# A float32 encoder trunk: the weight tiles' splits are issued with two tiles in hand instead of one

## The chip, the cores and the metric

The kernel runs on one core of one Trainium2 chip. The metric is the device time of one execution in microseconds (us); where several executions were timed, their median is given. The core's engines are TensorE (PE in the profile, with its weight loads as PEld), VectorE (DVE), ScalarE (ACT), GpSimd (POOL) and SyncE (SP), which issues the transfers here.

## The reference

Two layers of a hybrid encoder run over 272 positions (256 tokens and 16 learned meta tokens) of width 2048, in float32. In each layer one projection `h @ w_in` gives queries, keys, values and gates for two groups of heads. Four heads do gated linear attention in both directions, with a decay that depends on the data. Sixteen heads do neighbourhood attention over a grid 64 wide, with the meta tokens as further keys. Both outputs go through `w_out`, a residual and a layer norm; then a squared-ReLU MLP of width 8192, a residual and a second layer norm follow:

```python
mix = jnp.einsum('blm,md->bld', jnp.concatenate([y_gla, y_na], axis=-1), w_out)
h = _layer_norm(DEEPNORM_ALPHA * h + mix, ln1_w, ln1_b)
ff = jnp.einsum('blf,fd->bld', jnp.square(jax.nn.relu(jnp.einsum('bld,df->blf', h, w_ff1))), w_ff2)
return _layer_norm(DEEPNORM_ALPHA * h + ff, ln2_w, ln2_b)
```

The meta tokens are dropped from the output. All weights together are read once from HBM, some 400 MB.

## The kernel before

The activations stand transposed in SBUF, features on the partitions and positions along the free dimension. Every large product is done in three matmuls of a rounded float32 type (fp32r): a weight tile w is split into a high part `wh` and the rest `wl`, the activations likewise into `xh` and `xl`, and wh·xh, wh·xl and wl·xh are added in PSUM.

**The weight stream.** `order` (L120) yields the 512 KB weight tiles (128 x 1024) in the order of their use, 768 in all. `made` (L137) brings in one: SP issues its transfer into `raw` (L146), ACT casts it to `wh` (L147), DVE subtracts to get `wl` (L148). `raw`, `wh` and `wl` each rotate over three buffers (the pool `wst`). So the `wh` and `wl` of a tile cannot be written before PE has done with the tile three earlier, and a tile's transfer not before the splits of the tile three earlier are done. `weights` (L131) is called each time a new tile is needed. It first fills the queue `ready` up to a count by calling `made`, then hands out the oldest. The very first tile comes in four parts and the second in two (`first` in L122).

**The two loops of matmuls.** `by_m` (L190) works on one block of 128 output features at a time, eight blocks of the contraction to a weight tile; the three matmuls are in `three` (L151; L160 to L162, or L156 and L157 where 256 positions allow xh and xl to go side by side in one matmul of 512 columns). `by_k` (L173) keeps four blocks of outputs in PSUM and goes along the contraction two blocks at a time, 24 matmuls to a weight tile (L186). It serves where activations come in one after another: at the start of the program (`load_x`, L291, loads and splits two blocks of x ahead of each tile), at the output projection, and after a layer norm (`normed`, L872, which calls `renew`, L877, to split the normalized blocks).

**Work in the background.** Attention, gates and layer norms are generators in two queues, `bg` and `fg`. `pump` (L104) moves them on by some steps after each weight tile. A step's instructions are traced inside `issue_after(self.wl)` (L98): what a step puts on DVE is kept behind the DVE instruction that made the latest `wl`. The linear attention of a head (`gla_head`, L437) goes through nine levels. For most of them POOL forms differences (L463), ACT exponentials (L468), DVE a product (L469), and PE small matmuls (L498, L493); copies under a mask (L515) gather the results. The gates' reciprocals (L423) and products (L426) run beside them on DVE.

**The order on the engines.** The program is written through a framework whose scheduler orders each engine's instructions by a model of its own. Engines run their lists in that order. On SP the order is that of the transfers' issue.

## Time and profile before

| | |
|---|---|
| median of 3 runs | 2422.17 us (2421.37 to 2422.31) |
| the profiled execution | 2421.64 us |
| its span, first to last instruction | 2419.7 us |
| granted TensorE clock | 0.999 |
| PE, PEld busy | 99%, 94% of the span |
| DVE, ACT, POOL busy | 65%, 49%, 12% |
| HBM traffic | 412.34 MB read, 171 GB/s over the span |

The span is the profiled execution's time without some 2 us around it. A busy share is the time in which at least one instruction of the engine ran. Rows of a timeline give the start and the duration in us, the engine and line, the operation, the tiles written and read, and in brackets the idle time before it and who ended it. Rows of the waits name who waited for whom, the sum in us, the number of waits and the longest.

### The profile page before, as it was taken

Reading aid. Unit: us, or ns where it says so; the run is one execution under the profiler, and the core shown is the slowest. Engines: PE = TensorE matmul, PEld = TensorE weight load, DVE = VectorE, ACT = ScalarE, POOL = GpSimd, SP = SyncE. Lnnn points to the kernel's source line nnn. Section 1 sums busy time; section 2 is a strip of 40 time slices with the busy share of each in tenths; the row PEclk is TensorE's granted clock in tenths of the full one; section 3 lists DMA queues with packets and bytes.
Section 4 is the critical chain, followed back from the end, with each engine's and each line's share of the span. In section 5 each row is a group of like instructions: output and inputs, shape, how many; then the busy total and the mean of one; then the engine's idle time right before and its main releaser. Section 6 shows DMA issues by size and latency. Waiting matters only on the chain.

```text
span 2419.7 us, 43687 instructions
## 1 busy us (share of the span) xinstructions
PE 2399.3 (99%) x17582; PEld 2265.2 (94%) x17582; DVE 1570.8 (65%) x2475; ACT 1191.4 (49%) x1980; POOL 287.2 (12%) x448
## 2 busy tenths in 40 slices
PE   9999999999999999999999999999999999999998
PEld 9999999999999999999999889998988888888887
DVE  6678777775544455546577787778866555666655
ACT  6555555564433344444456555555644333444444
POOL 1165320010000000000020444300200000000000
PEclk9999999999999999999999999999999999999999
DMA  7534444555555555555555444456556556555554
GB/s 240 166 132 152 141 139 157 173 176 176 175 177 175 176 175 175 175 174 174 175 169 185 140 154 158 137 156 199 183 185 190 186 189 188 186 189 186 187 188 139
DMA packets 118362, 417.28 MB, mean 172 GB/s; under 512 B 13388, under 2 KB 16460, under 8 KB 118160
## 3 DMA queue, kind: packets, MB, share of 16 engines
q1 hardware_dynamic: 118160, 414.49, 53.9%
q8 instruction: 138, 2.26, 0.4%
q14 instruction: 64, 0.52, 0.1%
HBM read 412.34 MB, written 2.10 MB: 171 GB/s over the span
## 4 chain that ended last, share of the span: by engine, by line
PE 94%; DVE 3%; ACT 1%; POOL 1%; issue 1%; DMA 0%; ACTq 0%; SPq 0%; POOLq 0%; DVEq 0%
PE mm L156 22%; PE mm L160 17%; PE mm L162 17%; PE mm L161 17%; PE mm L157 11%; PE mm L186 6%; POOL lev L463 1%; DVE wl L148 1%; PE bg L498 1%; PE bg L651 1%; PE bg L600 0%; PE bg L541 0%; PE bg L324 0%; PE bg L542 0%; DVE acc L870 0%
## 5 line engine op out<-in xcount | busy, mean ns | idle before, releaser
L148 DVE TENSOR_TENSOR wl<-raw,wh 128x1024 fp32r<-128x1024 f32 (+1 forms) x772 | 947.0, 1227 | 655.4 <-ACT wh L147 645.8
L147 ACT CAST wh<-raw 128x1024 fp32r<-128x1024 f32 (+1 forms) x772 | 805.2, 1044 | 949.8 <-PE mm L161 401.6
L160 PE MATMUL mm<-x,wh 128*128 128x272 f32 (+2 forms) x2176 | 632.3, 291 | 0.0
L162 PE MATMUL mm<-x,wl 128*128 128x272 f32 (+2 forms) x2176 | 628.0, 289 | 0.0
L161 PE MATMUL mm<-x,wh 128*128 128x272 f32 (+2 forms) x2176 | 627.7, 288 | 0.0
L160 PEld LDWEIGHTS mm<-x,wh 128*128 128x128 f32 x2176 | 412.7, 190 | 3.2 <-issue 0.4
L162 PEld LDWEIGHTS mm<-x,wl 128*128 128x128 f32 x2176 | 410.1, 188 | 0.3
L156 PE MATMUL mm<-x,wh 128*128 128x512 f32 x1152 | 409.6, 397 | 0.0
L161 PEld LDWEIGHTS mm<-x,wh 128*128 128x128 f32 x2176 | 409.4, 188 | 0.0
L157 PE MATMUL mm<-x,wl 128*128 128x256 f32 x1152 | 324.6, 282 | 0.4 <-DVE wl L148 0.4
L156 PEld LDWEIGHTS mm<-x,wh 128*128 128x128 f32 x1152 | 217.5, 189 | 50.8 <-issue 0.4
L156 PE MATMUL mm<-y,wh 128*128 128x512 f32 x688 | 242.1, 393 | 0.0
L157 PEld LDWEIGHTS mm<-x,wl 128*128 128x128 f32 x1152 | 217.4, 189 | 1.3 <-DVE wl L148 1.1
L162 PE MATMUL mm<-y,wl 128*128 128x272 f32 (+1 forms) x720 | 207.6, 288 | 0.0
L160 PE MATMUL mm<-y,wh 128*128 128x272 f32 (+1 forms) x720 | 207.5, 288 | 0.0
L161 PE MATMUL mm<-y,wh 128*128 128x272 f32 (+1 forms) x720 | 207.2, 288 | 0.0
L157 PE MATMUL mm<-y,wl 128*128 128x256 f32 x688 | 193.0, 281 | 0.5 <-DVE wl L148 0.5
L463 POOL TENSOR_TENSOR lev<-be 128x128 f32<-128x128 f32 (+1 forms) x256 | 162.3, 665 | 109.4 <-PE bg L498 32.1
L156 PE MATMUL mm<-u,wh 128*128 128x512 f32 x496 | 174.9, 393 | 0.0
L156 PEld LDWEIGHTS mm<-y,wh 128*128 128x128 f32 x688 | 128.8, 187 | 29.5
L162 PE MATMUL mm<-u,wl 128*128 128x272 f32 (+1 forms) x528 | 152.2, 288 | 0.0
L160 PE MATMUL mm<-u,wh 128*128 128x272 f32 (+1 forms) x528 | 152.2, 288 | 0.0
(266 smaller groups left out, 3305.5 us busy)
## 6 DMA issues: line engine op xcount, KB each, us to landing
raw<-in_wff SPq DMA_DIRECT2D x512, 512.0 KB, 3.5
raw<-in_win SPq DMA_DIRECT2D x190, 512.0 KB, 3.6
raw<-in_wout SPq DMA_DIRECT2D x64, 512.0 KB, 3.6
nb<-in_nab SPq DMA_DIRECT2D x16, 352.0 KB, 3.9
out<-acc SPq DMA_DIRECT2D x8, 256.0 KB, 2.6
xraw<-in_xT SPq DMA_DIRECT2D x7, 272.0 KB, 5.1
wraw<-in_wup SPq DMA_DIRECT2D x2, 392.0 KB
raw<-in_win SPq DMA_DIRECT2D x4, 128.0 KB, 3.0
```

What stands on the lines that cost most here:

```text
L147: nc.scalar.copy(wh[:, c], raw[:, c])
L148: self.wl = nc.vector.tensor_tensor(wl[:, c], raw[:, c], wh[:, c].bitcast(F32), ALU.subtract).ins
L156: mm(ps, lhsT=wh[:, c:c + P], rhs=x.both[:, :, :T], start=first, stop=False)
L157: mm(ps[:, T:], lhsT=wl[:, c:c + P], rhs=xh[:, :T], start=False, stop=last)
L160: mm(o, lhsT=wh[:, c:c + P], rhs=xh[:, :n], start=first, stop=False)
L161: mm(o, lhsT=wh[:, c:c + P], rhs=xl[:, :n], start=False, stop=False)
L162: mm(o, lhsT=wl[:, c:c + P], rhs=xh[:, :n], start=False, stop=last)
L186: self.nc.tensor.matmul(ps[m][:, :n], lhsT=parts[p][0][:, c:c + P], rhs=acts[j][parts[p][1]][:, :n], start=j + p == 0, stop=j == nk - 1 an ...
L463: tt = lambda o, x, y: nc.gpsimd.tensor_tensor(o, x, y, ALU.subtract)
L498: nc.tensor.matmul(ps[b * 64:b * 64 + 64, s * 64:s * 64 + 64], lhsT=k[:, c:c + 64], rhs=q[:, r:r + 64], start=True, stop=True)
L651: nc.tensor.matmul(r[hs], lhsT=(v2 if rest else v1)[:, t, hs], rhs=p2[:, t, :] if rest else p1[:, 2 * t + hh, :], start=rest, stop=not rest)
```

## The change

`weights` fills `ready` up to three tiles instead of two before it hands out the oldest. So when tile i is handed out, tile i+2 has had its transfer, its cast and its subtraction issued, where before it was tile i+1. Buffers and everything else are as they were.

```diff
     def weights(self):

-        while len(self.ready) < 2:
+        while len(self.ready) < 3:
             self.ready.append(self.made(*next(self.stream, (None, 0))))
         return self.ready.popleft()
```

In the order in which the two programs are built, no instruction is added and none is gone. At the start, SP issues the third weight tile ahead of the second pair of x blocks; before, it came behind it. On DVE, 148 of the 772 subtractions L148 have another place, 143 of them an earlier one, and what they overtake is work of the background. On PE, some 15 of the 72 groups of level matmuls (L498, L493) stand up to 28 matmuls later.

## The prediction

> **What bounds the kernel now.** I read the page first, for the engine that is never free and for the costs of the lines that the change moves.

> ```profile
> span 2419.7 us, 43687 instructions
> PE 2399.3 (99%) x17582; PEld 2265.2 (94%) x17582; DVE 1570.8 (65%) x2475; ACT 1191.4 (49%) x1980; POOL 287.2 (12%) x448
> L148 DVE TENSOR_TENSOR wl<-raw,wh 128x1024 fp32r<-128x1024 f32 (+1 forms) x772 | 947.0, 1227 | 655.4 <-ACT wh L147 645.8
> L147 ACT CAST wh<-raw 128x1024 fp32r<-128x1024 f32 (+1 forms) x772 | 805.2, 1044 | 949.8 <-PE mm L161 401.6
> ```

> PE is busy for all but 2419.7 - 2399.3 = 20.4 us. One tile's split costs ACT 1.04 us and DVE 1.23 us. So I asked next what PE waits for: the waits of PE, all rows, and one of its weight loads.

> ```profile
> PE mm L186 <- ACT wh L147: 4.8, 1, 4.8
> PE bg L498 <- DVE lev L469: 1.6, 2, 1.3
> PE bg L541 <- ACT Am L529: 1.3, 1, 1.3
> PE mm L186 <- DVE wl L148: 1.0, 1, 1.0
> PE mm L157 <- DVE wl L148: 0.9, 2, 0.5
> PE bg L636 <- DVE nv L628: 0.6, 2, 0.3
> PE bg L651 <- DVE p L641: 0.6, 1, 0.6
> PE bg L498 <- ACT lev L468: 0.5, 1, 0.5
> PE bg L523 <- DVE lev L482: 0.4, 1, 0.4
> PE bg L636 <- DVE ns L587: 0.4, 2, 0.2
> PE bg L493 <- DVE lev L469: 0.2, 1, 0.2
> PEld mm L157 <- DVE wl L148: 2.1, 3, 1.0
> ```

> The first row is the start of the program. The others sum to 7.5 us, and only 1.0 + 0.9 of it is a wait for a split. That is the size of the question: the whole prize is a few us in 2420. Last, the windows of the two MLP stretches, and who holds the splits up:

> ```profile
> 480.00:1235.00 755.00, 755.00 (x6004) 754.79 (x6003) 412.72 (x528) 329.83 (x459) 12.63 (x8) 1.00 0.55 175
> 1690.00:2404.00 714.00, 714.00 (x4268) 633.42 (x4267) 436.08 (x592) 321.65 (x432) 13.12 (x8) 1.00 0.58 184
> ACT wh L147 <- PE mm L161: 401.6, 231, 2.6
> ACT wh L147 <- PE mm L156: 243.7, 148, 2.8
> DVE wl L148 <- ACT wh L147: 645.8, 527, 3.8
> ```

> In 755 + 714 = 1469 us PE has no idle time at all (columns: length, then busy PE, PEld, DVE, ACT, POOL). And ACT's cast there waits for PE: it stands ready before PE has left the buffer, which is the tile three back. With three buffers the split already starts at the earliest moment that exists. Issuing it earlier changes nothing in these stretches; it can only act where DVE or ACT have other work in front of the split.

> **The change part by part.** No instruction is added; places change. There are four terms.

> *1. The start: +1.3 us.* SP now issues the third weight tile ahead of the second pair of x blocks. Timelines of SP and ACT before, and PE by windows (length, busy, count):

> ```profile
> 4.51 0.43 SPq L295 DMA_DIRECT2D xraw<-in_xT  x1
> 4.99 0.43 SPq L146 DMA_DIRECT2D raw<-in_win  x1
> 9.80 0.74 ACT L209 CAST x<-xraw 128x272 fp32r<-128x272 f32 x2 [0.88 <-DMA xraw<-in_xT]
> 11.10 1.05 ACT L147 CAST wh<-raw 128x1024 fp32r<-128x1024 f32 x1 [0.56 <-DMA raw<-in_win]
> 4.77:10.20 5.43, 5.42 (x24) 1.00 0.93 289
> 10.20:31.50 21.30, 21.30 (x170) 1.00 0.89 305
> ```

> The 24 matmuls of the first tile end at 10.2. The second tile's need the pair of blocks whose transfer ended ACT's wait at 9.80 and whose first cast is done at half of 0.74 us later, 10.2: just in time, with no slack. The weight tile behind it in the queue landed at 11.10. With the two swapped, the same bytes stand ahead of the pair, so I let it land when the tile did: PE's second tile starts 11.10 - 9.80 = 1.3 us later. No one makes that up, for PE then runs without a gap, at 21.30/170 = 125 ns a matmul. Bounds: 0, if the two transfers share the queue so that the pair lands as before; 2.4, if ACT's cast of that weight tile (1.05), which now stands ahead of the pair's casts, comes fully in the way as well (1.3 + 1.05). I take 1.3, the distance of the two landings. [...]

> *2. Splits that PE waits for in the attention and layer norm of the second layer: -1.5 us.* These two rows of PE's timeline are the row "0.9, 2" above:

> ```profile
> 1425.57 0.39 PE L157 MATMUL mm<-x,wl 128*128 128x256 f32 x1 [0.36 <-DVE wl L148]
> ...
> 1629.57 0.38 PE L157 MATMUL mm<-y,wl 128*128 128x256 f32 x1 [0.55 <-DVE wl L148]
> ```

> In the changed order these two subtractions stand 2.6 and 3.6 us of DVE's work earlier, which is more than the wait. So they go. They cost at least the idle time, 0.9, and at most the weight loads' wait, 2.1; I take the middle.

> *3. From the first layer to the second: 0.* Here DVE is saturated, and order alone cannot make time:

> ```profile
> 1261.52 1.21 DVE L148 TENSOR_TENSOR wl<-raw,wh 128x1024 fp32r<-128x1024 f32 x1
> ...
> 1265.63 0.99 DVE L210 TENSOR_TENSOR x<-acc,x 128x272 fp32r<-128x272 f32 x2
> 1268.64 0.78 DVE L210 TENSOR_TENSOR x<-acc,x 128x272 fp32r<-128x272 f32 x2
> 1269.35 1.43 DVE L148 TENSOR_TENSOR wl<-raw,wh 128x1024 fp32r<-128x1024 f32 x1
> ```

> PE's wait of 1.0 is for the last of these. In the changed order it stands before the first pair of x halves. So the wait goes, but those halves, which PE takes at once, come one split (1.2) later. One wait replaces the other: 0, bounds -1.2 and +1.2. Late next are the x halves.

> *4. The levels of the linear attention: +0.7 us.* A background step's DVE work is tied behind the latest `wl`, which is now one tile further on. The worst case of before, DVE and PE:

> ```profile
> 1359.05 0.95 DVE L423 RECIPROCAL rs<-rs 128x128 f32<-128x128 f32 x1 [1.76 <-POOL rs L414]
> 1360.92 1.43 DVE L469 TENSOR_TENSOR lev<-lev,qk 128x512 f32<-128x512 f32 x2
> 1361.70 0.45 PE L498 MATMUL bg<-lev 128*64 128x64 f32 x8 [1.31 <-DVE lev L469]
> 1362.55 0.39 PE L156 MATMUL mm<-x,wh 128*128 128x512 f32 x1
> 1362.89 0.39 PE L156 MATMUL mm<-x,wh 128*128 128x512 f32 x1
> L469 DVE TENSOR_TENSOR lev<-lev,qk 128x512 f32<-128x512 f32 (+1 forms) x64 | 48.6, 762 | 10.7 <-ACT lev L468 10.2
> 1345.00:1437.00 92.00, 89.31 (x622) 76.31 (x620) 79.33 (x128) 56.11 (x113) 58.60 (x95) 1.00 0.45 147
> ```

> In the changed order one more product (1.43/2 = 0.7) and one split (1.2) stand between that reciprocal and the product that PE waits for: 1.9 later. The matmuls are also put behind four more pairs of L156 and L157, and the two rows of L156 give 0.34 us a pair: 1.4 later. So that wait grows by 0.5. I went through all 64 products of L469 in this way, from the end of each to the start of its matmuls: most had 2 to 7 us in hand and keep 1 to 5, some five come out 0.2 to 0.7 worse, two better by 0.2 and 0.7. I take +0.7. The waits of PE for levels above are 1.6 + 0.5 + 0.4 + 0.2 = 2.7 in 5 cases; bounds: -2.7 if all go, +6.1 if each grows by a whole split (5 x 1.23).

> SP's transfers go out as their buffers come free, with the splits; POOL's list differs by a few places. Both cost nothing while PE's MLP stretches show no wait. At the end of the program no tile is left to bring in, so the last layer norm is as it was.

> Sum: 1.3 - 1.5 + 0 + 0.7 = +0.5 us. The profiled execution took 2421.64, so 2422.1 in its terms; it lies 0.5 below the median of the runs, and against the median the forecast is 2422.17 + 0.5 = **2422.7**. Bounds of all terms together: 0 - 2.1 - 1.2 - 2.7 = -6.0 and 2.4 - 0.9 + 1.2 + 6.1 = +8.8.

> **The rivals.**

> *Nothing but the start (2422.17 + 1.3 = 2423.5).* The change does not split earlier at all, because the buffers decide, and the freed waits come back elsewhere on DVE. For it: the cast's 401.6 + 243.7 us of waiting for PE. Against: 143 subtractions do stand earlier.

> *Slower by more than 0.2%: DVE is held up in the attention.* DVE takes its list in order. A split that stands earlier, while PE has not left the tile three back, stops DVE, and the levels wait behind it. It decides from the point at which DVE has no room: it is busy 79.33 of 92 us in that window, so one more wait of 1.23 us in each 9 would fill it. Price: the five level waits grow by a split each, +6.1, the start +1.3, the two splits -0.9: +6.5, 2428.7. Against: in most levels there is room.

> *Faster by more than 0.2%:* the x pair lands as before (0), and every wait for a split or a level goes: -1.5 - 1.0 - 2.7 = -5.2, 2417.0. Against: levels are put behind more DVE work, not less.

> *The clock falls back at the start.* PE's first 24 matmuls take 5.43/24 = 226 ns, later ones 125. If the new pause of 1.3 us made it start cold again for as long, that is 24 x 0.101 = 2.4 us more: 2425.1. Against: after the pause of 1.31 us at 1361.70 pairs follow at 0.34 us, full speed. [...]

> **How the numbers follow.** A measurement of this kernel can tell about 0.2% (4.8 us) from no change: under 2417.3 is faster, over 2427.0 slower. Chances: the forecast 0.60, nothing but the start 0.22, the clock 0.04 (all three within 0.2%: 0.86), held up 0.10, faster 0.04. The range is 2419.0 to 2427.0: upward it takes in the first three cases with the start's upper bound and half of that of the levels, downward the lower bounds of the first three terms, and it leaves out the two ends.

> **What would show it.** Right: ACT's cast of the second pair of x blocks starts near 11.1 and PE's second tile near 11.5; no wait of PE for L148 near 1425 and 1629; at the second layer's first L186 a wait for L210 instead of L148; PE busy again near 2399; both MLP windows without a gap. Wrong: PE's waits for L469 summing to over 5 us, new gaps in the MLP, or the first L186 tiles at over 200 ns a matmul after 11 us.

## The result, and the profile after

The changed kernel takes **2433.86 us** (median of 5 executions, 2433.5 to 2434.05), the kernel before 2421.99 beside it: ratio 1.0049, 95% interval 1.0034 to 1.0064. It is slower by 11.9 us; the forecast was 0.5 slower, with a range that ended at 2427.0.

The page of the changed kernel, profiled in an execution of 2433.86 us; these are the rows that were shown first of the kernel before:

```profile
span 2431.9 us, 43690 instructions
PE 2404.6 (99%) x17582; PEld 2268.4 (93%) x17582; DVE 1562.0 (64%) x2475; ACT 1191.6 (49%) x1980; POOL 278.2 (11%) x448
L148 DVE TENSOR_TENSOR wl<-raw,wh 128x1024 fp32r<-128x1024 f32 (+1 forms) x772 | 944.6, 1224 | 684.3 <-ACT wh L147 674.0
```

The span grew by 12.2 us, in two parts: PE idle 2431.9 - 2404.6 = 27.3 against 20.4 (+6.9), and PE busy for 5.3 longer with the same 17582 matmuls. DVE's subtractions cost what they did, 1.22 us each. What changed is the last column: DVE stood idle ahead of them, waiting for the cast, for 674.0 us instead of 645.8.

PE's waits in the changed kernel (sum in us, number, longest):

```profile
PE bg L498 <- DVE lev L469: 7.1, 6, 2.1
PE mm L186 <- ACT wh L147: 5.1, 1, 5.1
PE bg L493 <- DVE lev L469: 1.8, 2, 1.3
PE bg L541 <- ACT Am L529: 1.8, 1, 1.8
PE mm L186 <- ACT x L209: 1.5, 2, 0.9
PE mm L186 <- DVE wl L148: 0.5, 1, 0.5
PE mm L186 <- DVE x L210: 0.4, 1, 0.4
```

The waits for level products are 7.1 + 1.8 = 8.9, where levels cost 2.7 before: +6.2 of the +6.9 of idle time. There are eight such waits now, five before. L157's waits for `wl` are gone.

Windows of the changed kernel (length, then busy PE, PEld, DVE, ACT, POOL, granted clock, DMA):

```profile
480.00:1235.00 755.00, 755.00 (x6003) 754.79 (x6003) 414.77 (x532) 330.22 (x460) 11.36 (x8) 1.00 0.58 175
1690.00:2404.00 714.00, 714.00 (x4258) 632.84 (x4257) 440.88 (x601) 326.03 (x440) 11.53 (x8) 1.00 0.62 187
1345.00:1437.00 92.00, 86.77 (x606) 74.29 (x606) 70.93 (x122) 52.51 (x106) 53.71 (x88) 0.98 0.45 134
```

Neither MLP stretch shows a gap or another clock. Each large matmul was matched with the same one of the kernel before, and the lag is how much later it starts. It is 1.6 us at 75 us, 6.5 after the first layer's attention (317), still 6.5 at 1213, 7.3 at 1290, 13.2 after the second layer's attention (1555), and 12.5 from 1634 to the end. So the start gives 1.6, the attention of the first layer 4.9 and that of the second 5.9. In the third window DVE is *less* busy than before (70.93 against 79.33), PE too, and the clock is at 0.98: nothing is saturated there. Something waits.

DVE's waits in the first layer's attention (110 to 367 us), before:

```profile
DVE wl L148 <- ACT wh L147: 17.9, 23, 3.0
DVE lev L481 <- ACT lev L480: 8.5, 4, 3.2
DVE lev L469 <- ACT lev L468: 5.9, 6, 2.5
```

and in the changed kernel:

```profile
DVE wl L148 <- ACT wh L147: 32.1, 28, 3.0
```

Before, DVE waited 8.5 + 5.9 us for exponentials with a product next in its list: the product ran the moment its operand was there. In the changed kernel these two rows are 0.6 and nothing: DVE waits for casts in their place, and the products come behind the subtraction. In the second layer the groups of lines show the same. DVE from 1345 to 1437 us, before (busy, mean ns, idle time ahead):

```profile
L148 DVE TENSOR_TENSOR wl<-raw,wh 128x1024 fp32r<-128x1024 f32 x26 | 33.5, 1292 | 3.2 <-ACT wh L147 3.1
```

and changed:

```profile
L148 DVE TENSOR_TENSOR wl<-raw,wh 128x1024 fp32r<-128x1024 f32 x24 | 30.2, 1257 | 9.5 <-ACT wh L147 9.4
```

One such case in full, ACT and then DVE of the changed kernel:

```profile
1375.49 0.63 ACT L468 ACTIVATE lev<-lev 128x512 f32<-128x512 f32 x1 [2.59 <-POOL lev L463]
1376.03 1.03 ACT L147 CAST wh<-raw 128x1024 fp32r<-128x1024 f32 x1
```

```profile
1377.09 1.26 DVE L148 TENSOR_TENSOR wl<-raw,wh 128x1024 fp32r<-128x1024 f32 x1 [1.68 <-ACT wh L147]
1378.27 0.94 DVE L423 RECIPROCAL rs<-rs 128x128 f32<-128x128 f32 x1
1379.13 0.62 DVE L469 TENSOR_TENSOR lev<-lev,qk 128x512 f32<-128x512 f32 x1
```

The exponential is done at 1376.12. Its product starts at 1379.13, 3.0 us later. DVE is idle for 1.68 us because the next instruction in its list is a subtraction whose cast stands on ACT behind that exponential, and the exponential itself waited 2.59 for POOL. Of the product's 3.0 us, 0.97 are this wait, 1.2 the subtraction and 0.9 a reciprocal. Followed on, the delay reaches PE at 1382.96 with a wait of 0.52; the products in between had room.

The other waits of PE for a level, followed back in the same way, are not all of this kind. Those of 1.29 us at 141.45 and of 1.66 at 309.59 come through casts that DVE waited for, 2.92 us at 135.84 and 2.30 at 299.41. Those of 0.97 at 1371.51 and of 0.87 at 1541.19 come through a subtraction's work, with no wait for its cast. Ahead of the longest, 2.07 us at 1423.36, DVE waits for something else. Two waits of DVE, the first on the way to 309.59, the second on the way to 1423.36:

```profile
299.41 1.23 DVE L148 TENSOR_TENSOR wl<-raw,wh 128x1024 fp32r<-128x1024 f32 x1 [2.30 <-ACT wh L147]
...
1421.47 0.42 DVE L170 TENSOR_TENSOR jn<-jn,mm 128x256 f32<-128x256 f32 x1 [1.97 <-ACT jn L169]
```

The copy L169 stands on ACT behind an exponential that waits for POOL, and POOL has worked on differences from 1408.17 to 1419.77 without a pause. The levels were late before that: POOL's work began behind a chain of DVE's in which three subtractions stand. So a subtraction ahead of the levels costs its wait in some places and its work in others, and both put off POOL's next differences.

### The profile page after: what moved, and what is told of

Read it like the earlier page. It is cut to its first block, busy times and chain, and to the rows that moved or that the text cites. A ratio compares the mean times of both kernels' runs of the same rounds, so it can differ in the third digit from the quotient of the medians.

```text
span 2431.9 us, 43690 instructions
## 1 busy us (share of the span) xinstructions
PE 2404.6 (99%) x17582; PEld 2268.4 (93%) x17582; DVE 1562.0 (64%) x2475; ACT 1191.6 (49%) x1980; POOL 278.2 (11%) x448
## 4 chain that ended last, share of the span: by engine, by line
PE 92%; DVE 3%; POOL 2%; ACT 1%; issue 1%; DMA 0%; SPq 0%; ACTq 0%; POOLq 0%; DVEq 0%
PE mm L156 21%; PE mm L160 17%; PE mm L162 17%; PE mm L161 17%; PE mm L157 11%; PE mm L186 5%; POOL lev L463 1%; DVE wl L148 1%; PE bg L498 1%; PE bg L651 1%; ACT wh L147 1%; PE bg L600 0%; DMA raw<-in_win 0%; ACT ns L583 0%; PE bg L541 0%
## 5 line engine op out<-in xcount | busy, mean ns | idle before, releaser
L148 DVE TENSOR_TENSOR wl<-raw,wh 128x1024 fp32r<-128x1024 f32 (+1 forms) x772 | 944.6, 1224 | 684.3 <-ACT wh L147 674.0
L147 ACT CAST wh<-raw 128x1024 fp32r<-128x1024 f32 (+1 forms) x772 | 805.4, 1044 | 953.8 <-PE mm L161 414.3
L161 PE MATMUL mm<-x,wh 128*128 128x272 f32 (+2 forms) x2176 | 628.3, 289 | 0.0
L161 PEld LDWEIGHTS mm<-x,wh 128*128 128x128 f32 x2176 | 409.9, 188 | 0.1
L156 PE MATMUL mm<-x,wh 128*128 128x512 f32 x1152 | 409.6, 397 | 0.0
L157 PE MATMUL mm<-x,wl 128*128 128x256 f32 x1152 | 324.5, 282 | 0.0
L156 PEld LDWEIGHTS mm<-x,wh 128*128 128x128 f32 x1152 | 217.5, 189 | 50.9 <-issue 0.4
L156 PE MATMUL mm<-y,wh 128*128 128x512 f32 x688 | 242.3, 393 | 0.0
L157 PEld LDWEIGHTS mm<-x,wl 128*128 128x128 f32 x1152 | 217.4, 189 | 0.2
L161 PE MATMUL mm<-y,wh 128*128 128x272 f32 (+1 forms) x720 | 207.2, 288 | 0.0
L157 PE MATMUL mm<-y,wl 128*128 128x256 f32 x688 | 193.5, 281 | 0.0
L156 PE MATMUL mm<-u,wh 128*128 128x512 f32 x496 | 174.9, 393 | 0.0
L463 POOL TENSOR_TENSOR lev<-be 128x128 f32<-128x128 f32 (+1 forms) x256 | 150.7, 619 | 111.6 <-PE bg L498 41.8
L156 PEld LDWEIGHTS mm<-y,wh 128*128 128x128 f32 x688 | 129.0, 187 | 29.9
```

Source lines behind the costliest of these rows:

```text
L147: nc.scalar.copy(wh[:, c], raw[:, c])
L148: self.wl = nc.vector.tensor_tensor(wl[:, c], raw[:, c], wh[:, c].bitcast(F32), ALU.subtract).ins
L156: mm(ps, lhsT=wh[:, c:c + P], rhs=x.both[:, :, :T], start=first, stop=False)
L157: mm(ps[:, T:], lhsT=wl[:, c:c + P], rhs=xh[:, :T], start=False, stop=last)
L161: mm(o, lhsT=wh[:, c:c + P], rhs=xl[:, :n], start=False, stop=False)
L463: tt = lambda o, x, y: nc.gpsimd.tensor_tensor(o, x, y, ALU.subtract)
```

## The experiments

Line numbers in some of these kernels differ from before's by up to a dozen. "In hand" counts the queue before the oldest tile is handed out: three in the changed kernel, two before. Lags are those of the profiled execution against before's.

### Which stretch: three tiles in hand in one part of the program only

The four kernels share one edit and differ in where the count changes:

```diff
+        self.depth = 2
...
-        while len(self.ready) < 2:
+        while len(self.ready) < self.depth:
...
+                    self.depth = 3
```

Three from the end of the first `by_k` on:

> Two tiles stay in hand until the first loop over x is through, three from there on; DVE's and PE's lists are those of the changed kernel but for the start. The traces set PE's second tile 1.6 us later with the change (0.3 of it at the very first matmul, 1.3 at the second tile). Theory A (the start costs 1.3 us, the attention nearly all the rest, because DVE stands at subtractions that wait for their cast): 2433.9 - 1.3 = 2432.5. Rival (the late start also shifts the phase of everything behind it, and a part of the attention's loss hangs on that phase): under 2430.

Measured 2433.07 (2430.63 to 2434.49), ratio 1.0045, interval 1.0033 to 1.0058: the rival falls. The lag is -0.1 us at 75 and at 110. Three in the first `by_k` only:

> Three tiles in hand only in the first loop over x, two from there on; the lists are those of before but for SP's, ACT's and DVE's first entries. Theory A: the start's term alone, 2422.0 + 1.3 = 2423.3, with PE's first wait for ACT's cast of x (L209, now line moved by two) near 0.9 us. Rival (phase): 2425 or more, with new waits for L469 in the attention.

Measured 2424.89 (2423.01 to 2426.32), 1.0011, 1.0002 to 1.002. That lies between the two, nearer to the rival's number, but not by its cause: the waits for L469 are as before, and the lag is 2.0 us at 12.5 us and 2.0 at the end, so all is lost at the start. Three only while linear and neighbourhood attention run in the background:

> Three tiles in hand only from the first background step of the linear attention to the end of the neighbourhood attention, two elsewhere. Theory A: 2422.0 + 8.5 to 9.5 = about 2431, with PE's waits for L469 near 9 us in sum. Rival (the layer norms and the way from the first layer to the second carry a good part): 2426 or less.

Measured 2432.04 (2430.78 to 2434.0), 1.0043, 1.003 to 1.0055, and PE's waits for level products sum to 8.9 us, as the theory had it. And the rest, from the end of the first layer's attention on and without the second's (the stretch between the start and the first attention has two in hand here; in the first of the four kernels it had three, and gave no lag):

> The complement: three tiles in hand from the end of the first loop over x, but two in the attention. Theory A: terms 2 and 3 of the prediction alone, within 1.5 us of before, 2421 to 2423.5; the MLP stretches without a gap in either. Rival (the layer norms and the way between the layers carry a good part of the loss): 2426 or more.

Measured 2421.91 (2421.39 to 2423.05), 1.0001, 0.9992 to 1.001. The attention carries some 10 us by itself, the start 1 to 4 (3 in the median), the remaining three quarters of the program nothing.

### Which coupling: the tie of the background to `wl`

A background step's DVE work is kept behind the latest subtraction. Three in hand makes that the subtraction of a tile one further on, whose cast cannot start before PE has left the tile three back. Here the steps are tied to the tile before the latest, as they were, with three in hand:

```diff
-        while len(self.ready) < 2:
+        while len(self.ready) < 3:
...
+        self.wl = self.wls[-2]
```

(`made` puts each subtraction into the list `wls`.)

> Three tiles in hand, but a background step's work on DVE is kept behind the subtraction of the tile one earlier than the newest, as it was before the change. Theory T (the tie is the cause: the levels' DVE work is forced behind a subtraction that is one tile further on): start term alone, 2422 + 1.5 = 2423.5, DVE's waits for the cast in the attention back near before's 33 us. Rival P (the earlier place in the program alone moves the subtraction ahead; the tie only adds to it): 2428 or more.

Measured 2425.59 (2425.11 to 2428.41), 1.0018, 1.0009 to 1.0027: between the two. The lag is 2.0 us at 12.5 us, more than the theory's start, and 4.0 at the end. With no tie at all, at three and at two:

```diff
-                with self.tc.issue_after(self.wl):
-                    next(q[0])
+                next(q[0])
```

> Three tiles in hand and no tie at all: the scheduler alone places the background. Theory T: 2423.5 or less, as with the old tie. Rival P: 2428 or more.

> Two tiles in hand, as before the change, and no tie. It is the control of the run above: what the tie is worth in itself. Theory T (the levels gain from every place ahead of a subtraction): 2420 to 2422. Rival (without the tie the subtraction falls behind the background and PE waits for it): 2425 or more, PE's waits for L148 well over before's 1.9 us.

Measured 2428.79 (2427.18 to 2429.67), 1.0029, 1.0017 to 1.004, and 2422.97 (2422.15 to 2423.3), 1.0005, 0.9996 to 1.0013. The tie is not needed for before's time, but without it three in hand still costs about 6 us, as rival P had it: the subtraction's earlier place costs something without any tie. The lag is 3.3 us after the start, where the profile has half clock from 11.98 us for 3.41, and 6.6 at the end, so that place is worth some 3 here. The old tie once more, with the start at two:

> Three tiles in hand, but two during the first 16 tiles, and the background steps tied behind the subtraction of the tile before the latest, as before. Theory (the tie carries most of the attention's loss, the subtraction's new place the rest; the start apart): the version with the old tie throughout, 2425.6, less its start of 1.3 to 2: 2423.5 to 2424.5. Rival (the tie alone is the cause): 2421.8 to 2422.5, as before.

Measured 2423.59 (2423.05 to 2424.08), 1.0008, 0.9999 to 1.0017. Against 2433.07 with the new tie and the same start, the tie carries 9.5 us; some 2 remain over before (the lag at the end is 2.0), as the theory had it and not its rival, though the interval just reaches 1. DVE's idle time ahead of L148 while the levels run (from the first product L469 of a layer to its last, both layers) goes with it: 22.6 us before, 47.5 in the changed kernel, 29.4 and 29.2 with the old tie.

### Which instruction: transfer and cast ahead, subtraction in its old place

```diff
-        while len(self.ready) < 2:
+        while len(self.ready) < 3:
...
+        for t in list(self.ready)[:2]:
+            self.rest(t)
```

(`made` then ends with the cast; `rest` makes the subtraction when the tile is the second in `ready`, and the tie follows it.)

> Transfer and cast of a tile are issued with three tiles in hand, the subtraction and the tie with two. Theory D (only DVE's list decides: the subtraction's place): the start's 1.5 us and nothing else, 2423.5. Rival (earlier transfers and casts disturb ACT's exponentials or the memory): 2427 or more.

Measured 2423.08 (2422.83 to 2424.69), 1.0007, 0.9998 to 1.0016. The same with the start at two:

> Transfers and casts go three tiles in hand after the first 16 tiles; each subtraction, and the tie of the background to it, stays two tiles in hand as before. Theory (only the subtraction's place costs): with the start as before nothing is left of the loss, and casts that are done early save DVE almost nothing, since its waits for casts were 22.4 against 22.6 us: 2421.5 to 2422.5. Rival (casts and transfers ahead help the attention, hidden so far by the start's 1.1): 2419 to 2421.

Measured 2421.49 (2420.89 to 2421.83), 0.9999, 0.999 to 1.0008. Casts and transfers three ahead cost nothing beyond the start, and bring nothing. DVE's idle time ahead of L148 is 22.4 in both. So the attention's loss comes with the place of the subtraction on DVE and of the work that is tied behind it.

### Its work or its wait: casts and subtractions in halves

If what stands in front of the levels is the subtraction's 1.22 us of work, cutting it in two changes nothing. If it is the wait for the cast, half of the cast ends the wait.

```diff
-            nc.scalar.copy(wh[:, c], raw[:, c])
-            self.wl = nc.vector.tensor_tensor(wl[:, c], raw[:, c], wh[:, c].bitcast(F32), ALU.subtract).ins
+            for c in (slice(c.start, (c.start + c.stop) // 2), slice((c.start + c.stop) // 2, c.stop)) if parts == 1 else (c,):
+                nc.scalar.copy(wh[:, c], raw[:, c])
+                self.wl = nc.vector.tensor_tensor(wl[:, c], raw[:, c], wh[:, c].bitcast(F32), ALU.subtract).ins
```

> The changed kernel with each tile's cast and subtraction in two halves of 512 columns; transfers, buffers and order of tiles as in the change. DVE then waits only for the first half of the cast, and subtracts it while ACT casts the second. Theory (the price in the attention is DVE's waiting for casts, 47.5 us against 22.6): the wait of a moved subtraction falls from about 1.04 us to about half, so half of the attention's 10 us comes back: 2427 to 2430. Rival (the price is the subtraction's place and work alone, in front of the levels): nothing comes back, and the longer sum of two halves costs something more: 2434 to 2437.

> The kernel before with the same halves, as the measure for the other: what the halves cost or bring where the subtraction stands in its old place. Both theories: 2421 to 2423.5, since most casts of before are done or under way when DVE comes to the subtraction, and the MLP hides ACT's and DVE's additional fixed costs. If it is itself several us faster or slower than 2422, only the difference between the two counts.

The changed kernel with halves: 2424.2 (2423.75 to 2426.25), 1.0012, 1.0003 to 1.0021. Before with halves: **2418.45** (2417.61 to 2421.26), 0.9988, 0.9979 to 0.9996. The difference between the two orders falls from 11.9 to 5.75 us, by some half. DVE's and PE's waits of the changed kernel with halves, from 110 to 367 us:

```profile
DVE wl L149 <- ACT wh L148: 24.2, 27, 2.8
PE bg L499 <- DVE lev L470: 1.5, 2, 0.9
PE bg L494 <- DVE lev L470: 0.9, 1, 0.9
```

The wait for casts falls from 32.1 to 24.2 although a tile now takes DVE 2 x 0.69 = 1.39 us instead of 1.22; in the order of before it is 15.1 with halves and 17.9 without. So the moved subtractions add 9.1 us of waiting where they added 14.2. The lag of the changed kernel with halves against before with halves grows by 2.9 us in the first attention and by 2.3 in the second, where whole tiles gave 4.9 and 5.9. (Both profiled executions are the slowest of their eleven; the clock was at half from 14.03 in the first and from 1293.12 in the second, outside the stretches compared.) So about half of the attention's price came back, as the theory had it, and the rival, that nothing does, falls. The time is below the theory's 2427 because finer pieces on both engines also gave before 3.3 us, which neither theory had; whether a shorter wait or a smaller piece of work is what pays is not separated by this pair. Hence quarters on before:

```diff
+            for c in [slice(q, q + 256) for q in range(0, size, 256)] if parts == 1 else (c,):
```

> The kernel before with each tile's cast and subtraction in four quarters of 256 columns. From the half (0.62 us a cast, 0.69 us a subtraction) and the whole (1.04, 1.23), a quarter takes about 0.41 and 0.43 us. Theory that DVE's waiting for casts is what counts: the first wait falls by another 0.2 us, but each tile takes DVE 0.33 us and ACT 0.4 us more than in halves, which in the attention is as much again: 2418 to 2421, no better than halves. Rival (finer is better, since other work of ACT and DVE comes between the parts sooner): 2415 to 2417.

Measured 2421.1 (2419.65 to 2423.79), 0.9998, 0.9989 to 1.0007: finer still is not better, 0.1 above the upper end that the theory gave. Halves in the old order are the only version here that is clearly faster than the kernel before, by 0.12%. 1.8 us of that are made in the first attention; where the rest is made, the trace of its profiled execution does not settle, since that one was the slowest of its eleven.

### The clock after short pauses

The third window's clock of 0.98 was unexpected. Two pauses of PE in the changed kernel:

```profile
309.59 0.45 PE L498 MATMUL bg<-lev 128*64 128x64 f32 x8 [1.66 <-DVE lev L469]
...
1423.36 0.69 PE L498 MATMUL bg<-lev 128*64 128x64 f32 x8 [2.07 <-DVE lev L469]
```

and PE by windows behind them (length, busy, matmuls, granted clock), in the changed kernel:

```profile
312.00:316.00 4.00, 4.00 (x32) 0.74 0.36 131
...
1424.00:1428.00 4.00, 4.00 (x27) 0.65 0.27 78
```

The same stretches with the start as before, whose attention has the same order:

```profile
312.00:316.00 4.00, 4.00 (x49) 1.00 0.26 105
1424.00:1428.00 4.00, 4.00 (x37) 1.00 0.47 147
```

PE is busy in all four, but at 0.74 and 0.65 it does 32 and 27 matmuls where it did 49 and 37 (not the same ones: the second kernel is some 2 to 3 us ahead). The clock record of the changed kernel holds 0.5 for 3.41 us from 310.66 and again from 1423.41: 1.7 us of PE's time each, 3.4 together. The same matmuls fall 1.5 us behind those of the second kernel in each stretch. The first 1.5 stays to the end; of the second, 1.3 is made up at 1437, since the second kernel waits 1.1 us for a level at 1433.66 and the changed one does not. To measure that by itself, before was given pauses in the first MLP, where it has no gap:

```diff
+            for _ in range(PAUSE.get(self.tiles, 0)):
+                nc.scalar.copy(wh[:, :512], raw[:, :512])
```

> The kernel before, with 19 deliberate pauses of PE in the MLP of the first layer, where it otherwise has no gap: at every tenth tile ACT repeats half of the cast 7 to 20 times (0.6 us each), so that PE waits 0.3 to 8 us for that one tile. It measures by itself what a pause does to the granted clock. Theory (a pause of about 1.7 us or more can halve the clock for 3.4 us, as seen after 1.66 and 2.07 us but not after 1.31 and 1.79): no fall below 1.3 us, a fall after some of the pauses from 1.5 to 3 us, after all of the longer ones. Rival (only an idle window of about 3.4 us does it, and the falls seen had another cause, such as thin work before the pause): falls only behind pauses above 3.4 us here. Each fall costs 3.41 us at half clock, 1.7 us.

It took 2566.66 us; its pauses came out longer than meant, most of them 2.46 to 9.63 us. PE by windows, behind a pause of 2.46 us that ends at 562.88 and one of 3.40 that ends at 599.01:

```profile
560.00:564.00 4.00, 1.20 (x8) 1.00 0.00 0
564.00:568.00 4.00, 3.86 (x19) 0.57 0.54 174
568.00:572.00 4.00, 4.00 (x34) 1.00 0.60 222
...
598.00:601.00 3.00, 1.99 (x7) 0.53 0.00 0
601.00:605.00 4.00, 4.00 (x20) 0.50 0.92 292
605.00:609.00 4.00, 4.00 (x33) 1.00 0.38 113
```

The pause of 2.46 us was enough, so the rival, that only a window idle throughout does it, falls. Pauses from 2.46 us up were all followed by half clock, those of up to 1.32 us, where nothing longer stood near, by none; between 1.4 and 2.4 it made none. All stretches at half clock in this run are 3.41 us or a multiple of it, but for the one that the program's end cuts off, and all begin on one grid of 3.413 us.

## Why the prediction was wrong

*What bounds the kernel* stood: no gap in either MLP, and the version with three in hand outside start and attention takes 2421.91. (By the order in the two traces 176 of the 772 subtractions stand earlier on DVE, not 143; nothing above rests on the number.)

*Term 1, the start, +1.3.* Right in size; the lag at 75 us is 1.6, of which 0.3 are there at the first matmul already. ACT, and then PE, in the changed kernel:

```profile
10.18 1.05 ACT L147 CAST wh<-raw 128x1024 fp32r<-128x1024 f32 x1 [1.27 <-DMA raw<-in_win]
11.13 0.73 ACT L209 CAST x<-xraw 128x272 fp32r<-128x272 f32 x2
```

```profile
11.60 0.77 PE L186 MATMUL mm<-x,wh 128*128 128x272 f32 x4 [0.92 <-ACT x L209]
```

The forecast had 11.1 and 11.5. That it met them so closely is partly luck, for the 1.3 us are made up otherwise than it said. It let the pair land at 11.1, where the tile had landed. By the trace's record the tile now lands at 10.16 and the pair at 10.83 (9.78 before), and the last 0.3 is ACT's cast of the tile, which stands ahead of the pair's and which the forecast had only in its upper bound. The pair landed 0.67 us behind the tile, where the forecast had it land with it. The start alone costs more in the median (2424.89, from 2423.01 up), and the profiled executions of the version without a tie and of the changed kernel with halves show half clock from 11.98 and 14.03 for 3.41 us. So the rival of the clock does happen at the start, in some executions. PE's pauses there are 2.41 and 1.77 us, longer than the 1.3 of the forecast; it was excluded from one pause of 1.31 us that left the clock alone.

*Term 2, the two splits, -1.5.* They went: no wait of L157 for `wl` is left, and the lag falls by 0.8 from 1555 to 1634. That is the lower bound, the idle time.

*Term 3, the second layer's start, 0.* Right within its bounds: the waits there are now for `x` (L209, L210) and `wl`, and the lag moves from 6.5 to 7.3.

*Term 4, the levels, +0.7.* **This step failed.** It counted a subtraction that moves ahead of a product as 1.23 us of work, and set that against the product's slack, one product at a time. The subtraction brought its own wait along: its cast, which waits for PE's buffer and, in ACT's order, for exponentials that wait for POOL (from 110 to 367 us ACT's casts L147 waited 30.5 us for PE's L161, and its exponentials L468 43.6 for POOL). The case at 1379 shows the size: 2.2 us of its 3.0 are the subtraction's, wait and work, where 1.2 had been counted; over both layers DVE waits 24.9 us more ahead of subtractions while the levels run. The delays also add up from level to level, as on the way to 1423.36, and that was left out too. The bound of that term, +6.1, was about what came in idle time, +6.2, but by luck: it stood for five waits that grow by a split each, and eight came. The other omission is what came of the clock behind those longer waits (0.5 for 3.41 us behind 1.66 and behind 2.07): 3.4 us of PE's time, about half of which stayed in the span. Idle time 6.9 and clock 3.4 make 10.3 of the span's 12.2. The remaining 1.9 are longer busy time of PE at full clock; the version with the start as before, whose profile has no half clock, shows it as well (PE busy 2401.5, idle 2428.7 - 2401.5 = 27.2). In both, PE goes from large matmuls to those of the background 183 times, before 175; what makes the rest of it is open.

*The rivals.* "DVE is held up in the attention" is what happened, with a chance of 0.10 and a price of 2428.7. Its mechanism was written down rightly (DVE stops at a split whose buffer PE has not left, and the levels queue behind it). It was set aside by "in most levels there is room", which came from the same products priced without the wait, and its condition, that DVE have no room left, was wrong: DVE's busy time in the window fell. DVE, which took its list in order (the product at 1379.13 had been ready since 1376.12), was late here without being short of time. Its price, 2428.7, again counted a split's work for each wait; 2433.86 came. The named sign of error, waits for L469 of over 5 us, came with 8.9. A fourth buffer, with which the cast would not wait for the tile three back, was not tried.

## What to carry to other kernels

When an instruction moves forward on an engine that runs its list in order, as DVE did here (it stood idle until 1377.09 for a subtraction's cast, with the product behind it ready at 1376.12), price it by the time at which its operands are ready, not by its duration: what stands behind it inherits that wait, and so does what is tied to it. Here transfers and casts could be moved ahead without cost or gain, the start apart, and what cost time was the place of the instruction that waits for them. Where such an instruction must stand early, try producer and consumer in halves: here that gave 9.7 us in the changed order and 3.3 in the old one, and quarters gave nothing over whole tiles. And a pause of the matmul engine of about 2 us could cost 1.7 us more than its length here: those of 1.66 and 2.07 us were each followed by 3.41 us at half clock.
